# Branch A's scores by pairs of query tiles, the low term as 64-row products

## The chip, the cores and the metric

The kernel runs on one core of a Trainium2 chip. TensorE multiplies, VectorE, ScalarE and GpSimd do the elementwise work, and the DMA queues bring data in and out. The metric is the time of one execution on the device in microseconds; for the kernel before it is 2207.16 us, the median of three runs (2205.43 to 2207.44).

## The reference

One encoder layer is applied to two sequences, a prompt of 1024 tokens and a sample of 512, with 1024 features. All arrays are float32.

```
xn = rmsnorm(x);  z = xn @ W_in -> q_A k_A v_A q_B k_B v_B gate_A gate_B
branch A: 8 query heads of 64, 2 key/value heads; q, k normalised per head and rotated
    s = q @ k.T / 8;  p = softmax(s);  o_A = p @ v          (every query sees every key)
branch B: 8 heads, a window of 8 x 16 neighbours on a grid 64 wide, with a learned bias
mix = (sigmoid(gate_A) * (o_A @ W_pA) + sigmoid(gate_B) * (o_B @ W_pB)) @ W_out
x = x + mix;  x = x + relu(rmsnorm(x) @ W_up)^2 @ W_down;  y = rmsnorm(x)
```

The change touches only `s = q @ k.T` of branch A.

## The kernel before, in words

**Precision.** TensorE multiplies in a reduced form of float32 (fp32r). The kernel keeps accuracy by splitting each operand into a high part, rounded to that form, and a low part, the rest. An ordinary product is then three TensorE products (`mm3`, L157 to L159: high by high, high by low, low by high), summed in PSUM.

**Branch A's operands.** A head has only 64 features, and a product can contract over 128 partitions, so the split is laid out along the partitions. For each key/value group `g` and 128-token tile `tt`, `heads_t` transposes the rotated heads (L446) into a PSUM tile `pt`: four query heads in two 128-partition blocks, and the key head twice, in both halves of the third block. From it ScalarE and VectorE write

- `qT[e]` (e = head's parity): the high part in partitions of half `e` (L451, ScalarE), the low part in the other half (L454, VectorE);
- `kT[:, 0]`: the high part of the keys, in both halves (L452); `kT[:, 1]`: the low part of the keys, in both halves (L460).

**Scores.** One product of `qT[e]` with `kT[:, 0]` over all 128 partitions therefore gives (q high + q low) by k high, and one with `kT[:, 1]` gives (q high + q low) by k low. `s_tile(u, j)` does this for one unit `u` (a head and a block of 512 queries) and one of its four query tiles `j`. It takes a score buffer of two PSUM banks from a pool of two (`big`), and for each block of 512 keys (two of them for the prompt, one for the sample) issues L563 (against the high part, `start=True`) and L564 (against the low part). Then VectorE takes the row maximum (L566), ScalarE the exponential with the row sum (L569), VectorE the reciprocal (L571) and GpSimd scales the probabilities (L572).

**Order of the work.** Units are pipelined: while unit `u` has its probabilities transposed (L606, four 128-column transposes for each 128 keys `kc`), split (L611 ScalarE, L612 VectorE) and multiplied with the values (L582, L583), the score tiles of the next unit are issued at `kc` 0, 1, 3 and 4 of 8 for the prompt and 0, 0, 1 and 2 of 4 for the sample. The products of gate A (L157 to L159, `gpss`) are pulled in between as filling work. This is the order in which the source issues the work; a scheduler then sorts the instructions of each engine anew, by its own estimates, so that the order on an engine can differ.

The sample comes first, then the prompt; each has two key/value groups, so there are four stretches with branch A's scores. Branch B, the projections and the two-layer network follow and are not touched.

Of the kernel before, what the change touches and what calls it, by code (L numbers as in the profile page):

```python
# [10 lines left out]
F32 = mybir.dt.float32  # L11
F32R = mybir.dt.float32r
BF16 = mybir.dt.bfloat16
AF = mybir.ActivationFunctionType
ALU = mybir.AluOpType
AX = mybir.AxisListType

P = 128
D = 1024
NC8 = D // P  # L20
HD = 64
# [39 lines left out]
def encoder(ctx: ExitStack, tc: tile.TileContext, xs, outs, w):  # L61
    nc = tc.nc
    dram = ctx.enter_context(tc.tile_pool(name="dram", bufs=1, space=bass.MemoryType.DRAM))
    cst = ctx.enter_context(tc.tile_pool(name="cst", bufs=1))
    sml = ctx.enter_context(tc.tile_pool(name="sml", bufs=8))
# [17 lines left out]
    def phase(name, bufs=2):  # L83
        return tc.tile_pool(name=name, bufs=bufs, reuse_waits="tile")

    def slot(shape, dt, name, left=False):
        return (s8l if left else s8r).tile(shape, dt, tag="s8", name=name)
# [4 lines left out]
    def mm(name):  # L92
        return pmm.tile([P, 512], F32, tag="mm", name=name)

    def big(name):
        return pbig.tile([P, 1024], F32, tag="big", name=name)
# [40 lines left out]
    def bias_row(r):  # L137
        nc.sync.dma_start(biases[r], shifted[:, :, 7 - r : 23 - r, :])
# [187 lines left out]
    def run(tr, nxt, first):  # L326
        N, x, T, NT, NB = tr.N, tr.x, tr.T, tr.NT, tr.NB
# [8 lines left out]
        fill = Fill()  # L336
# [70 lines left out]
        def load_v(g, alloc):  # L407
            return load_cols(win, 1792 + 256 * g, 256, f"v{N}_{g}", alloc)

        early = {}  # L410
        for g in range(2):
            with phase(f"phR{N}_{g}") as ph:
# [23 lines left out]
                qT = [slot([P, 2, T], F32R, f"qT{N}_{g}_{i}") for i in range(2)]  # L436
                kT = slot([P, 2, T], F32R, f"kT{N}_{g}")
# [3 lines left out]
                def heads_t(tt):  # L441
                    nm = f"{N}_{g}_{tt}"
                    pt = big(f"pq{nm}")[:, :384].rearrange("p (b q) -> p b q", q=P)
                    rrf = rr_of.pop(tt).rearrange("p h d -> p (h d)")
                    for b in range(3):
                        nc.tensor.transpose(pt[:, b, :], rrf[:, b * P : (b + 1) * P], ident)  # L446
                    ts_ = slice(tt * P, (tt + 1) * P)

                    half = (slice(0, HD), slice(HD, P))
                    for e in range(2):  # L450
                        nc.scalar.activation(qT[e][half[e], :, ts_], pt[half[e], 0:2, :], AF.Copy)  # L451
                    nc.scalar.activation(kT[:, 0, ts_], pt[:, 2, :], AF.Copy)  # L452
                    for e in range(2):
                        nc.vector.tensor_tensor(  # L454
                            qT[e][half[1 - e], :, ts_],
                            pt[half[e], 0:2, :],
                            qT[e][half[e], :, ts_].bitcast(F32),
                            op=ALU.subtract,
                        )
                    nc.vector.tensor_tensor(kT[:, 1, ts_], pt[:, 2, :], kT[:, 0, ts_].bitcast(F32), op=ALU.subtract)  # L460
# [15 lines left out]
                for tt in range(NT):  # L476
                    tb, j = divmod(tt, 4)
                    nm = f"{N}_{g}_{tt}"
# [24 lines left out]
                    if tt >= 2:  # L503
                        heads_t(tt - 2)
                    sq = ph.tile([P, 5, HD], F32, tag="sq", name=f"sq{nm}", bufs=1)
                    zq = z[:, :320].rearrange("p (h d) -> p h d", d=HD)
                    ss = sml.tile([P, 8], F32, tag="ss", name=f"ssA{nm}")
# [12 lines left out]
                    u = ph.tile([P, 5, HD], F32, tag="u", name=f"u{nm}", bufs=2)  # L520
# [3 lines left out]
                    for e in range(2):  # L524
# [4 lines left out]
                            op=ALU.mult,  # L529
# [12 lines left out]
                if g == 0:  # L542
                    warm_table(AF.Exp, rr[:, 0, 0:1], f"e{N}")
                values(NT - 1)
                heads_t(NT - 2)
                fill.pull(6)
                heads_t(NT - 1)

            if first and g == 0:
                setup_bias()  # L550
            with phase(f"phA{N}_{g}") as ph:
                units = [(h, qb) for h in range(4) for qb in range(NB)]
                PP = {}

                def s_tile(u, j):
                    h, qb = u
                    nm = f"{N}_{g}_{h}_{qb}_{j}"
                    q0 = (qb * 4 + j) * P
                    lhs = qT[h % 2][:, h // 2, q0 : q0 + P]
                    s = big(f"s{nm}")[:, :T]  # L560
                    for kb in range(NB):
                        ks = slice(kb * 512, kb * 512 + 512)
                        nc.tensor.matmul(s[:, ks], lhs, kT[:, 0, ks], start=True, stop=False)  # L563
                        nc.tensor.matmul(s[:, ks], lhs, kT[:, 1, ks], start=False, stop=True)  # L564
                    nm_ = sml.tile([P, 1], F32, tag="nm", name=f"nm{nm}")
                    nc.vector.tensor_reduce(nm_, s, axis=AX.X, op=ALU.max, negate=True)  # L566
                    p = ph.tile([P, T], F32, tag="P", name=f"p{nm}", bufs=8)
                    l = sml.tile([P, 1], F32, tag="l", name=f"l{nm}")
                    nc.scalar.activation(p, s, AF.Exp, bias=nm_, accum_out=l)  # L569
                    rl = sml.tile([P, 1], F32, tag="rl", name=f"rl{nm}")  # L570
                    nc.vector.reciprocal(rl, l)  # L571
                    nc.gpsimd.tensor_scalar(p, p, rl, 1.0, op0=ALU.mult, op1=ALU.mult)  # L572
                    PP[u, j] = p

                o_of = {}

                def pv(u, kc, hi, lo):
                    h, qb = u
                    if kc == 0:
                        o_of[u] = mm(f"o{N}_{g}_{h}_{qb}")  # L580
                    o = o_of[u]
                    nc.tensor.matmul(o, vhl[:, kc, :], hi, start=(kc == 0), stop=False)  # L582
                    nc.tensor.matmul(o, vhl[:, kc, :], lo, start=False, stop=(kc == NT - 1))  # L583
                    if kc == NT - 1:
                        r0 = (g * 4 + h) * HD
                        finish_o(o, 512, oad[r0 : r0 + HD, qb * 512 : qb * 512 + 512], ph, f"A{N}_{g}_{h}_{qb}")

                for j in range(4):
                    s_tile(units[0], j)
                    fill.pull(2)  # L590
                queue = []
                LAG = 2
                for ui, u in enumerate(units):
                    h, qb = u
                    if first:
                        bias_row(g * 4 + ui)
                        if g == 0 and ui == 1:
                            early["a"] = load_a(1)
                        if g == 0 and ui == 2:
                            early["v"] = load_v(1, slot)  # L600
                    nxt_u = units[ui + 1] if ui + 1 < len(units) else None
                    sdone = 0
                    for kc in range(NT):
                        pt = mm(f"pT{N}_{g}_{h}_{qb}_{kc}")
                        for j in range(4):
                            nc.tensor.transpose(  # L606
                                pt[:, j * P : (j + 1) * P], PP[u, j][:, kc * P : (kc + 1) * P], ident
                            )
                        hi = ph.tile([P, 512], F32R, tag="pth", name=f"pth{N}_{g}_{h}_{qb}_{kc}", bufs=3)
                        lo = ph.tile([P, 512], F32R, tag="ptl", name=f"ptl{N}_{g}_{h}_{qb}_{kc}", bufs=3)  # L610
                        nc.scalar.activation(hi, pt, AF.Copy)  # L611
                        nc.vector.tensor_tensor(lo, pt, hi.bitcast(F32), op=ALU.subtract)  # L612
                        queue.append((u, kc, hi, lo))
                        if nxt_u is not None:
                            while sdone < 4 and kc >= ((0, 1, 3, 4) if NB == 2 else (0, 0, 1, 2))[sdone]:
                                s_tile(nxt_u, sdone)
                                sdone += 1

                        fill.pull(1 if NB == 1 or kc % 4 < 3 else 0)
                        if len(queue) > LAG:  # L620
                            pv(*queue.pop(0))
                fill.drain()
                for item in queue:
                    pv(*item)
# [47 lines left out]
        with phase(f"phB{N}") as ph:  # L672
# [168 lines left out]
            units = [(h, j) for h in range(8) for j in (1, 2, 0, 3)]  # L841
            n = len(units)
            LS, LV = (1, 1) if NB == 2 else (2, 1)
            for i in range(n + LS + LV):
                if i < n - 8:
                    f = (5 if i < LS else 2 + i % 2) if NB == 1 else 5 + (i % 3 > 0)
                else:
                    f = 3 + i % 2 if NB == 1 else 7
# [31 lines left out]
        with phase(f"phG{N}") as ph:  # L880
# [25 lines left out]
            for c in range(NC8):  # L906
# [3 lines left out]
                for tb in range(NB):  # L910
# [4 lines left out]
                    nm = f"{N}_{c}_{tb}"  # L915
# [30 lines left out]
            for half in range(2):  # L946
                wo = wos[half]
                hc = slice(half * 512, half * 512 + 512)
                for tt in range(NT):
                    tb, j = divmod(tt, 4)  # L950
                    nm = f"{N}_{half}_{tt}"
# [35 lines left out]
                    if half == 1:  # L987
# [5 lines left out]
                        else:  # L993
# [6 lines left out]
                            if 3 <= tt <= 5:  # L1000
                                j = tt - 3
# [411 lines left out]
    for i, tr in enumerate(trunks):  # L1413
        run(tr, trunks[i + 1] if i + 1 < len(trunks) else None, i == 0)
# [66 lines left out]
```

## Time and profile before

| | |
|---|---|
| median of three runs | 2207.16 us (2205.43 to 2207.44) |
| the profiled execution | 2204.99 us |
| its span, first to last instruction | 2203.2 us |
| mean granted TensorE clock | 0.993 |
| score products, high keys (L563) | 160 |
| score products, low keys (L564) | 160 |
| transposes of probabilities (L606) | 640 |
| HBM traffic | 263.63 MB read, 87.88 MB written |

The profile shows one execution. The page gives the busy time of each engine, the span in slices and the costliest groups of instructions; further views give a group by line, the busy time of each engine in chosen stretches, the waits of an engine and single instructions in the order of time. PE is TensorE's products, PEld its weight loads, DVE VectorE, ACT ScalarE, POOL GpSimd. In the row of a group come the line in the kernel, the engine and operation, output and inputs by the program's names, the form, the count, the total busy time, the mean duration in ns, and the idle time of the engine ahead of it with what ended it. The record of a product reaches to its modelled end, and successive products overlap, so what a product costs in a stream is the distance between two starts.

### The profile page before, as it was taken

Reading aid. Unit: us, or ns where it says so; the run is one execution under the profiler, and the core shown is the slowest. Engines: PE = TensorE matmul, PEld = TensorE weight load, DVE = VectorE, ACT = ScalarE, POOL = GpSimd, SP = SyncE. Lnnn points to the kernel's source line nnn. Section 1 sums busy time; section 2 is a strip of 40 time slices with the busy share of each in tenths; the row PEclk is TensorE's granted clock in tenths of the full one; section 3 lists DMA queues with packets and bytes.
Section 4 is the critical chain, followed back from the end, with each engine's and each line's share of the span. In section 5 each row is a group of like instructions: output and inputs, shape, how many; then the busy total and the mean of one; then the engine's idle time right before and its main releaser. Section 6 shows DMA issues by size and latency. Waiting matters only on the chain. (4 is left out here: it accounts for less than half of the span.)

```text
span 2203.2 us, 32342 instructions
## 1 busy us (share of the span) xinstructions
PE 2141.6 (97%) x11168; PEld 1873.9 (85%) x11168; DVE 1458.0 (66%) x2823; ACT 1106.2 (50%) x2359; POOL 345.7 (16%) x453
## 2 busy tenths in 40 slices
PE   7999999999999999999999899999999999999998
PEld 7787777888898888888888699998999988888886
DVE  5665566667757755555782777777777777769563
ACT  4654553556636744545540465555655543433352
POOL 2232220333233213222200300003000000000000
PEclk9999999999999999999999999999999999999999
DMA  5535457521122123423463654468544699788561
GB/s 168 156 95 149 142 157 243 202 81 32 44 70 89 39 70 118 118 86 97 144 202 124 234 163 143 155 222 206 173 143 156 219 351 339 235 269 292 166 201 58
DMA packets 318442, 349.72 MB, mean 159 GB/s; under 512 B 31559, under 2 KB 254919, under 8 KB 318279
## 3 DMA queue, kind: packets, MB, share of 16 engines
q1 hardware_dynamic: 277927, 281.58, 40.8%
q10 hardware_dynamic: 35136, 50.61, 6.6%
q0 software_dynamic: 5216, 15.47, 2.5%
q8 instruction: 88, 1.44, 0.3%
q14 instruction: 75, 0.61, 0.1%
HBM read 263.63 MB, written 87.88 MB: 160 GB/s over the span
## 5 line engine op out<-in xcount | busy, mean ns | idle before, releaser
L159 PE MATMUL dn<-wd,al 128*128 128x512 f32 x624 | 242.8, 389 | 0.0
L158 PE MATMUL dn<-wd,ah 128*128 128x512 f32 x624 | 242.8, 389 | 0.0
L157 PE MATMUL dn<-wd,ah 128*128 128x512 f32 x624 | 242.7, 389 | 0.0
L1034 ACT ACTIVATE ah<-ar 128x512 fp32r<-128x512 f32 x168 | 104.4, 628 | 212.8 <-PE dn L158 196.0
L1035 DVE TENSOR_TENSOR al<-ar,ah 128x512 fp32r<-128x512 f32 x168 | 115.9, 698 | 77.1 <-ACT ah L1034 66.4
L157 PEld LDWEIGHTS dn<-wd,ah 128*128 128x128 f32 x624 | 117.1, 188 | 24.4
L159 PEld LDWEIGHTS dn<-wd,al 128*128 128x128 f32 x624 | 117.1, 188 | 24.3
L158 PEld LDWEIGHTS dn<-wd,ah 128*128 128x128 f32 x624 | 117.1, 188 | 24.2
L612 DVE TENSOR_TENSOR ptls<-pTs,pths 128x512 fp32r<-128x512 f32 x160 | 107.5, 686 | 38.1 <-ACT pths L611 37.6
L611 ACT ACTIVATE pths<-pTs 128x512 fp32r<-128x512 f32 x160 | 94.2, 598 | 74.9 <-PE pTs L606 72.9
L572 POOL TENSOR_SCALAR ps<-ps,rls 128x1024 f32<-128x1024 f32 (+1 forms) x96 | 96.1, 1003 | 215.0 <-DVE rls L571 208.6
L566 DVE TENSOR_REDUCE nms<-ss 128x1 f32<-128x1024 f32 (+1 forms) x96 | 99.5, 1040 | 26.3 <-PE ss L564 26.2
L144 POOL TENSOR_TENSOR rs_f<-ms_f,mhalf 128x1 f32<-128x1 f32 x12 | 7.4, 615 | 652.4 <-DVE ms_f L142 652.4
L157 PE MATMUL gpss<-xs_0h,w_gs 128*128 128x512 f32 x256 | 105.9, 414 | 3.0 <-ACT sgs L355 1.3
L569 ACT ACTIVATE ps<-ss,nms 128x1024 f32<-128x1024 f32 (+1 forms) x96 | 93.3, 973 | 23.7 <-DVE nms L566 21.3
L606 PEld LDWEIGHTS pTs<-ident,ps 128*128 128x128 f32 x640 | 78.1, 140 | 29.7 <-POOL ps L572 5.6
L159 PE MATMUL gpss<-xs_0h,w_gs 128*128 128x512 f32 x256 | 101.1, 395 | 0.1
L606 PE MATMUL pTs<-ident,ps 128*128 128x128 f32 x640 | 99.0, 274 | 2.0 <-DVE ptls L612 1.0
L158 PE MATMUL gpss<-xs_0l,w_gs 128*128 128x512 f32 x256 | 100.9, 394 | 0.0
L157 PE MATMUL ua<-B,A 128*128 128x384 f32 x256 | 86.4, 338 | 5.6 <-ACT A L1034 5.6
L783 POOL TENSOR_SCALAR pbs<-pbs,rlbs 128x384 f32<-128x384 f32 (+1 forms) x96 | 56.4, 592 | 225.3 <-DVE rlbs L782 219.1
L1034 ACT ACTIVATE A<-S 128x512 fp32r<-128x512 f32 x128 | 76.1, 623 | 28.5 <-DVE S L1079 25.8
(279 smaller groups left out, 6428.1 us busy)
## 6 DMA issues: line engine op xcount, KB each, us to landing
ar<-ud SPq DMA_DIRECT2D x120, 512.0 KB
br<-in_w_mlp_down_dram SPq DMA_DIRECT2D x72, 512.0 KB
rawu<-in_w_mlp_up_dram SPq DMA_DIRECT2D x64, 512.0 KB
ud<-c ACTq DMA_DIRECT2D x128, 192.0 KB
raw_gs<-in_w_in_dram SPq DMA_DIRECT2D x32, 512.0 KB
zgs<-sgs ACTq DMA_DIRECT2D x48, 256.0 KB
ud<-cs SPq DMA_DIRECT2D x64, 192.0 KB
raw_os<-in_w_out_dram SPq DMA_DIRECT2D x16, 512.0 KB
```

The lines of the kernel that those rows point to most:

```text
L157: nc.tensor.matmul(out, ah, bh, start=start, stop=False, **kw)
L158: nc.tensor.matmul(out, ah, bl, start=False, stop=False, **kw)
L159: nc.tensor.matmul(out, al, bh, start=False, stop=stop, **kw)
L566: nc.vector.tensor_reduce(nm_, s, axis=AX.X, op=ALU.max, negate=True)
L569: nc.scalar.activation(p, s, AF.Exp, bias=nm_, accum_out=l)
L572: nc.gpsimd.tensor_scalar(p, p, rl, 1.0, op0=ALU.mult, op1=ALU.mult)
L606: nc.tensor.transpose(pt[:, j * P : (j + 1) * P], PP[u, j][:, kc * P : (kc + 1) * P], ident)
L611: nc.scalar.activation(hi, pt, AF.Copy)
L612: nc.vector.tensor_tensor(lo, pt, hi.bitcast(F32), op=ALU.subtract)
L783: nc.gpsimd.tensor_scalar(p, p, rl, 1.0, op0=ALU.mult, op1=ALU.mult)
L1034: nc.scalar.activation(hi, src, AF.Copy)
L1035: nc.vector.tensor_tensor(lo, src, hi.bitcast(F32), op=ALU.subtract)
```

## The change

Each query tile now has its high and low parts in halves that depend on the parity of the tile as well as of the head: on odd tiles `d = e ^ 1`, so the high part lies in the other half. `s_tile` becomes `s_pair(u, jj)`, which handles query tiles `2*jj` and `2*jj + 1` at once, with both score buffers. It first issues the products against the high keys for both tiles, over all 128 partitions as before. Then, for each block of keys, it issues the products against the low keys for the two tiles in turn, each only over the 64 partitions that hold the tile's high query part: one tile's product uses partitions 0 to 63, the other's 64 to 127, and they write different PSUM banks. The product of the low query part with the low key part is no longer computed. The maximum, exponential, reciprocal and scaling follow for the one tile and then the other, as before. Pairs are issued at `kc` 0 and 3 of 8 for the prompt and 0 and 1 of 4 for the sample, and the filling work at the start of a stretch is pulled four steps after each pair instead of two after each tile.

```
                     for e in range(2):
-                        nc.scalar.activation(qT[e][half[e], :, ts_], pt[half[e], 0:2, :], AF.Copy)
+                        d = e ^ (tt & 1)
+                        nc.scalar.activation(qT[e][half[d], :, ts_], pt[half[e], 0:2, :], AF.Copy)
                     nc.scalar.activation(kT[:, 0, ts_], pt[:, 2, :], AF.Copy)
                     for e in range(2):
+                        d = e ^ (tt & 1)
                         nc.vector.tensor_tensor(
-                            qT[e][half[1 - e], :, ts_],
+                            qT[e][half[1 - d], :, ts_],
                             pt[half[e], 0:2, :],
-                            qT[e][half[e], :, ts_].bitcast(F32),
+                            qT[e][half[d], :, ts_].bitcast(F32),
                             op=ALU.subtract,
                         )
...
-                def s_tile(u, j):
+                def s_pair(u, jj):
                     h, qb = u
...
-                    for kb in range(NB):
-                        ks = slice(kb * 512, kb * 512 + 512)
-                        nc.tensor.matmul(s[:, ks], lhs, kT[:, 0, ks], start=True, stop=False)
-                        nc.tensor.matmul(s[:, ks], lhs, kT[:, 1, ks], start=False, stop=True)
...
+                    ss = []
+                    for j in (2 * jj, 2 * jj + 1):
+                        q0 = (qb * 4 + j) * P
+                        s = big(f"s{N}_{g}_{h}_{qb}_{j}")[:, :T]
+                        ss.append((j, q0, s))
+                        for kb in range(NB):
+                            ks = slice(kb * 512, kb * 512 + 512)
+                            lhs = qT[h % 2][:, h // 2, q0 : q0 + P]
+                            nc.tensor.matmul(s[:, ks], lhs, kT[:, 0, ks], start=True, stop=False)
+                    for kb in range(NB):
+                        ks = slice(kb * 512, kb * 512 + 512)
+                        for j, q0, s in ss:
+                            d = (h + j) % 2
+                            hs = slice(HD * d, HD * d + HD)
+                            nc.tensor.matmul(
+                                s[:, ks], qT[h % 2][hs, h // 2, q0 : q0 + P], kT[hs, 1, ks], start=False, stop=True
+                            )
...
-                for j in range(4):
-                    s_tile(units[0], j)
-                    fill.pull(2)
+                for jj in range(2):
+                    s_pair(units[0], jj)
+                    fill.pull(4)
...
-                            while sdone < 4 and kc >= ((0, 1, 3, 4) if NB == 2 else (0, 0, 1, 2))[sdone]:
-                                s_tile(nxt_u, sdone)
+                            while sdone < 2 and kc >= ((0, 3) if NB == 2 else (0, 1))[sdone]:
+                                s_pair(nxt_u, sdone)
                                 sdone += 1
```

More of the change, by code (lines that the diff above doesn't have):

```diff
@@ L553, in run @@
                 PP = {}
-                def s_tile(u, j):
+                def s_pair(u, jj):
                     h, qb = u
[L557 to L560, printed above, removed]
+                    ss = []
[7 more added lines that the diff above has]
+                            nc.tensor.matmul(s[:, ks], lhs, kT[:, 0, ks], start=True, stop=False)
@@ L561, in s_tile @@
                     for kb in range(NB):
                         ks = slice(kb * 512, kb * 512 + 512)
[L563 to L573, printed above, removed]
+                        for j, q0, s in ss:
[4 more added lines that the diff above has]
+                            )
@@ new lines, in s_pair @@
+                    for j, q0, s in ss:
+                        nm = f"{N}_{g}_{h}_{qb}_{j}"
+                        nm_ = sml.tile([P, 1], F32, tag="nm", name=f"nm{nm}")
+                        nc.vector.tensor_reduce(nm_, s, axis=AX.X, op=ALU.max, negate=True)
+                        p = ph.tile([P, T], F32, tag="P", name=f"p{nm}", bufs=8)
+                        l = sml.tile([P, 1], F32, tag="l", name=f"l{nm}")
+                        nc.scalar.activation(p, s, AF.Exp, bias=nm_, accum_out=l)
+                        rl = sml.tile([P, 1], F32, tag="rl", name=f"rl{nm}")
+                        nc.vector.reciprocal(rl, l)
+                        nc.gpsimd.tensor_scalar(p, p, rl, 1.0, op0=ALU.mult, op1=ALU.mult)
+                        PP[u, j] = p
```

## The prediction

> **What bounds the kernel now.** I read the page's busy shares first, then busy time by stretch, then TensorE's waits inside these stretches, then single products in the order of time.
>
> ```profile
> span 2203.2 us, 32342 instructions
> PE 2141.6 (97%) x11168; PEld 1873.9 (85%) x11168; DVE 1458.0 (66%) x2823; ACT 1106.2 (50%) x2359; POOL 345.7 (16%) x453
> ```
>
> TensorE is busy for 97% of the span. That is an average, so the stretches that hold branch A's scores come next. The score products come in four stretches, two key/value groups of the 512-token sequence and two of the 1024-token one; the row of their line gives the first and the last start, and the table the stretches.
>
> ```profile
> L563 PE MATMUL ss<-kTs,qTs x160: 387/397/501, 62.1 to 783.8; 128*128 128x512 f32 x160
> ...
> core 0: us, PE busy (x) PEld busy (x) DVE busy (x) ACT busy (x) POOL busy (x), PEclk, DMA share, GB/s
> 62.00:95.00 33.00, 32.40 (x158) 24.97 (x159) 25.39 (x56) 24.30 (x52) 9.71 (x14) 1.00 0.42 120
> 139.00:172.00 33.00, 32.34 (x162) 25.36 (x163) 24.55 (x53) 23.77 (x52) 10.83 (x16) 1.00 0.37 108
> 481.00:600.00 119.00, 117.81 (x628) 96.21 (x629) 88.28 (x139) 78.75 (x139) 36.88 (x32) 1.00 0.12 37
> 675.00:800.00 125.00, 124.91 (x670) 102.05 (x670) 90.86 (x143) 82.82 (x145) 36.75 (x32) 1.00 0.17 49
> sum 310.00, PE 307.46 PEld 248.58 DVE 229.08 ACT 209.63 POOL 94.17; mean PE 76.87 PEld 62.15 DVE 57.27 ACT 52.41 POOL 23.54
> ```
>
> TensorE is busy for 307.5 of 310 us at a granted clock of 1.00; VectorE and ScalarE have about a quarter to a third left. So in these stretches a microsecond added to or taken from TensorE moves the end by a microsecond, until another engine becomes late. The waits in the longest of them:
>
> ```profile
> engine line waited for: us in total, times, longest us
> PE ss L563 <- DVE kTs L460: 1.2, 1, 1.2
> PE pTs L606 <- DVE ptls L612: 1.0, 2, 0.7
> ```
>
> Two microseconds, none of it for a score buffer. What a product costs is not its record but the distance from its start to the next start:
>
> ```profile
> 744.72 0.39 PE L563 MATMUL ss<-kTs,qTs 128*128 128x512 f32 x1
> 744.73 0.19 PEld L564 LDWEIGHTS ss<-kTs,qTs 128*128 128x128 f32 x1
> 744.95 0.40 PE L564 MATMUL ss<-kTs,qTs 128*128 128x512 f32 x1
> 744.96 0.19 PEld L157 LDWEIGHTS gpss<-xs_0h,w_gs 128*128 128x128 f32 x1
> 745.19 0.39 PE L157 MATMUL gpss<-xs_0h,w_gs 128*128 128x512 f32 x1
> 745.42 0.40 PE L158 MATMUL gpss<-xs_0l,w_gs 128*128 128x512 f32 x1
> ...
> 746.11 0.58 PEld L606 LDWEIGHTS pTs<-ident,ps 128*128 128x128 f32 x4
> 746.34 0.60 PE L606 MATMUL pTs<-ident,ps 128*128 128x128 f32 x4
> 746.66 0.19 PEld L563 LDWEIGHTS ss<-kTs,qTs 128*128 128x128 f32 x1
> 746.69 0.48 PE L563 MATMUL ss<-kTs,qTs 128*128 128x512 f32 x1
> 746.77 0.19 PEld L564 LDWEIGHTS ss<-kTs,qTs 128*128 128x128 f32 x1
> 747.01 0.40 PE L564 MATMUL ss<-kTs,qTs 128*128 128x512 f32 x1
> ```
>
> Two things are to be seen. Products of 512 columns start every 0.23 us (744.72, 744.95, 745.19), though each record lasts 0.39: the last 0.16 us of one lies beside the next. And the weights of the next product are loaded while the present one runs (the load of 744.96 starts with the product of 744.95), so the 0.19 us of a load cost nothing.
>
> **The change part by part.** Durations that follow are means of these groups.
>
> ```profile
> L563 PE MATMUL ss<-kTs,qTs 128*128 128x512 f32 x160 | 68.4, 427 | 3.3 <-DVE kTs L460 3.3
> L564 PE MATMUL ss<-kTs,qTs 128*128 128x512 f32 x160 | 64.2, 401 | 0.0
> L606 PE MATMUL pTs<-ident,ps 128*128 128x128 f32 x640 | 99.0, 274 | 2.0 <-DVE ptls L612 1.0 <-POOL ps L572 0.3 <-DVE rls L571 0.2
> L566 DVE TENSOR_REDUCE nms<-ss 128x1 f32<-128x1024 f32 x64 | 77.7, 1217 | 16.5 <-PE ss L564 16.5
> L569 ACT ACTIVATE ps<-ss,nms 128x1024 f32<-128x1024 f32 x64 | 71.4, 1115 | 17.7 <-DVE nms L566 15.4 <-DVE rls L571 2.0
> L569 ACT ACTIVATION_READ_ACCUMULATOR ps<-ss,nms 128x1 f32 x96 | 19.0, 198 | 0.0
> L454 DVE TENSOR_TENSOR qTs<-pqs,qTs 64x256 fp32r<-64x256 f32 x48 | 20.3, 422 | 2.1 <-ACT kTs L452 1.4
> L451 ACT ACTIVATE qTs<-pqs 64x256 fp32r<-64x256 f32 x48 | 18.1, 377 | 5.0 <-PE pqs L446 3.4 <-DVE w_gs L152 1.3
> L740 DVE TENSOR_TENSOR kBs<-pkbs,kBs 64x512 fp32r<-64x512 f32 x48 | 33.1, 689 | 38.4 <-ACT kBs L738 37.9
> L738 ACT ACTIVATE kBs<-pkbs 64x512 fp32r<-64x512 f32 x48 | 28.5, 594 | 40.0 <-PE pkbs L159 30.9 <-DVE kBs L740 8.5
> ```
>
> *What stays.* The 160 first products (L563) and the 160 second products (L564) keep their number, their 512 columns and a weight load each; so do the reduces, exponentials and normalisations. The only work that can vanish is time shared by two of the 160 products that shrink from 128 to 64 rows. Run one at a time they would cost what they cost now, 160 x 0.23 = 36.8 us.
>
> *How many can share.* The scheduler sorts each engine's work, so I count in the order of TensorE's instructions of the built kernel. With T for a product on rows 0 to 63, B for rows 64 to 127, the 160 stand in 76 unbroken runs: 29 of one product, 10 of two on the same half, 13 TB, 11 of the form TBT and 13 TBTB. If neighbours on different halves run together, a TB or TBT run saves one place and a TBTB run two: 13 + 11 + 26 = 50 places, not the 80 that the source suggests. In the other cases the second buffer's first product, or another stage's, was sorted in between.
>
> *What a shared place saves.* At most the whole 0.23 us: 50 x 0.23 = 11.4 us (0.227 unrounded). At least nothing, if halves don't run side by side. Between these, the second product needs its own weights. The nearest row is the run of four transposes, each with a load of its own: (0.60 - 0.27) / 3 = 0.11 us from one to the next. I take it that the second product starts one such load later, so a place saves 0.23 - 0.11 = 0.12 us and 50 save 5.9 us. The Trainium skill (TensorE: Matmul & The Clock Gate, Part 3) has products on different row groups start about 4 ns apart; by that the 50 places would save about 11.2 us and the forecast would come out some 5 us lower. No run before the change has two products on different rows, so the trace neither agrees nor differs.
>
> *What a change of shape costs.* In the old kernel every product uses all 128 rows (the "128*128" in each row). Each of the 76 runs is entered from a 128-row product and left to one: 152 changes. No row shows such a change. Lower bound: the change between transposes and products, which costs nothing: after the four transposes of 746.34 the next two products start at 746.69 and 747.01, and 0.67 us for four transposes and one product is 4 x 0.11 + 0.23. A gain is excluded, since the plain 0.23 us is never beaten by products of 512 columns. Upper bound: the array runs empty (0.39 - 0.23 = 0.16 us) and the new weights are only loaded then (0.19 us), 0.35 us. I take 0.16 us: the tail is what two successive products of different shape would share in the array, which no row shows being shared, while the load goes into a place that the running product doesn't use, as the load of 744.96 does. That is 152 x 0.16 = 24.6 us (0.162 unrounded), with 0 and 53 us as ends.
>
> *Buffers.* A score tile fills one of two buffers, and now two tiles are filled nearly together. A buffer is free after reduce, exponential and accumulator read: 1.22 + 1.12 + 0.20 = 2.53 us, and the second of a pair waits for the first one's reduce, 3.75 us. Laying both kernels' TensorE orders out at 0.23 us a product and 0.11 us a transpose, the places where buffer or probabilities come too late add up to about 1.3 us before and 2.0 us after. Behind such a wait on TensorE's queue stand transposes, value products and gate products alike, so it costs in full: +0.7 us.
>
> *Query halves.* On odd tiles ScalarE's 24 copies (L451, 377 ns) write the other half of the partitions and VectorE's 24 subtractions (L454) read inputs on different halves. L738 and L740 do both already, at 594 and 689 ns for 64x512 against 377 and 422 for 64x256, which is no dearer per element. Nothing is added. DMAs, their queues and GpSimd's instructions keep their number.
>
> *Sum.* -5.9 + 24.6 + 0.7 = +19.4 us on the profiled execution's 2204.99 us. The median of the runs, 2207.16 us, lies 2.2 us above it; on that I forecast 2226.
>
> **The rivals.**
>
> *Sharing without a price (faster).* The 64-row products flow in behind the 128-row ones with no gap, as products do behind transposes. Then 5.9 to 11.4 us vanish: 2196 to 2201, say 2199. For it: TensorE is full in these stretches, so all of it would show. Against it: the rows show free succession only where the shape stays 128x128. It decides once a change of shape costs less than 5.9 / 152 = 0.04 us (0.07 if places save in full). The Trainium skill (TensorEngine Tiling (Array Packing), Key Properties) speaks against it: changing the tiling mode, unlike changing the tile, drains the engine, and it gives no time for that. No run here shows it yet.
>
> *Empty array and exposed load (much slower).* Nothing of the new shape is loaded before the old has left: 152 x 0.35 = 53 us, less 5.9, so about 2254. For it: a 64-row load and a 128-row load would have to sit in one spare set of weights. Against it: loads run well ahead wherever the trace can be looked at.
>
> *The halves do not run side by side and changes are free (same).* The order changes and nothing else: 2207 to 2208. The middle ground belongs here too, where price and saving cancel (0.04 to 0.07 us a change).
>
> *The buffers become the bound.* With both filled together, TensorE would stand before a pair, with VectorE's second reduce (1.22 us) as the cause. Across 48 pairs even half a microsecond each would be 24 us. Against it: the layout above leaves 2.5 us or more to nearly every reuse, and VectorE is busy 229 of 310 us. I count it within the forecast's spread.
>
> **How the numbers follow.** Below 0.2%, about 4.4 us, a difference can't be told from none here (the three runs span 2 us). Sharing without a price gets 0.31; no change and cancelling 0.13; the forecast, with 0.09 to 0.22 us a change, 2214 to 2236, 0.43; the dear change above it 0.13. So faster 0.31, same 0.13, slower 0.56. The range takes in the faster rival's low end and leaves the dearest changes out: 2196 to 2243, some 0.15 outside. The forecast's own range is 2214 to 2236.
>
> **What will show it.** In the order of time, pairs on different halves should start 0.11 us apart rather than 0.23 (a saved place), and the first 64-row product of a run, and the first 128-row one behind it, should start about 0.39 us after their forerunners rather than 0.23 (the price of a change). The four stretches should together take 19 us more, all else unchanged. If pairs start together and their neighbours stay at 0.23 us, the faster rival is right. If gaps exceed 0.5 us, loads are exposed. If TensorE's waits name L566's or L569's successor in front of score products for more than 3 us, the buffers were misjudged.

## The result, and the profile after

The changed kernel takes 2223.34 us (median of 6 runs, 2220.94 to 2228.24) against 2207.30 us of the kernel before beside it: a ratio of 1.0077, 95% interval 1.0067 to 1.0088. It is 0.8% slower. The forecast was 2226 us, slower.

The page's head for the changed kernel shows the same number of TensorE products and a span that is 16.0 us longer.

```profile
span 2219.2 us, 32334 instructions
PE 2161.5 (97%) x11168; PEld 1861.2 (84%) x11168; DVE 1459.5 (66%) x2823; ACT 1108.2 (50%) x2359; POOL 346.1 (16%) x453
```

Where the 16 us lie is shown by the four stretches, each from its first score product to its last product with the values. First the kernel before, then the changed one; after the bounds come the length and each engine's busy time with its instructions.

```profile
core 0: us, PE busy (x) PEld busy (x) DVE busy (x) ACT busy (x) POOL busy (x), PEclk, DMA share, GB/s
62.10:103.20 41.10, 40.58 (x201) 31.31 (x201) 31.13 (x66) 28.94 (x61) 11.07 (x16) 1.00 0.49 140
139.00:179.80 40.80, 40.05 (x201) 31.59 (x202) 29.49 (x60) 27.20 (x58) 12.11 (x17) 1.00 0.45 125
481.10:610.50 129.40, 128.31 (x686) 104.80 (x687) 93.61 (x146) 83.34 (x147) 36.88 (x32) 1.00 0.12 36
674.70:803.00 128.30, 128.17 (x685) 104.85 (x686) 91.95 (x144) 84.18 (x148) 37.39 (x33) 1.00 0.17 51
```

```profile
62.20:107.00 44.80, 44.78 (x206) 31.34 (x207) 31.21 (x66) 29.43 (x61) 11.08 (x16) 1.00 0.43 132
142.00:185.10 43.10, 43.02 (x201) 30.51 (x202) 29.42 (x60) 27.48 (x58) 13.23 (x17) 1.00 0.44 120
487.10:621.50 134.40, 134.14 (x686) 98.54 (x687) 94.28 (x146) 83.32 (x147) 36.07 (x32) 1.00 0.12 35
685.70:819.80 134.10, 134.00 (x685) 98.57 (x686) 93.10 (x144) 84.28 (x148) 37.58 (x33) 1.00 0.17 48
```

The stretches sum to 339.6 us before and 356.4 us after: +16.8 us, all of the difference and 0.8 more. The long stretches hold the same number of products (686 and 685; the first short one holds five more), the clock stays at 1.00, and VectorE and ScalarE keep their busy time. TensorE is busy throughout, but its weight loads are busy for less: in the third stretch 98.5 us instead of 104.8. Part of that is that loads overlap. The rows of the second score product's loads, before and after, show both that and a new idle time ahead of them:

```profile
L564 PEld LDWEIGHTS ss<-kTs,qTs 128*128 128x128 f32 x160 | 30.5, 190 | 3.5
L576 PEld LDWEIGHTS ss<-kTs,qTs 64*128 64x128 f32 x160 | 17.8, 184 | 22.3 <-issue 22.1
```

The 160 loads of 184 ns would fill 29 us one by one and fill 17.8. The idle time ahead of them grew from 3.5 to 22.3 us. The waits of the weight loads list it with the others of its kind (columns: who waited for whom, us in total, times, longest):

```profile
engine line waited for: us in total, times, longest us
PEld ss L576 <- issue: 22.1, 74, 0.4
PEld gpss L157 <- issue: 7.4, 24, 0.4
PEld os L598 <- issue: 4.6, 17, 0.4
```

L576 is the 64-row product. 74 times, and there are 76 runs, its load came after 0.30 us of idle time on average, in which it waited for nothing that the profile names. The groups of the two score products:

```profile
L570 PE MATMUL ss<-kTs,qTs 128*128 128x512 f32 x160 | 53.1, 412 | 3.3 <-DVE kTs L463 3.3
L576 PE MATMUL ss<-kTs,qTs 64*128 64x512 f32 x160 | 45.8, 466 | 0.0
```

And in the order of time, a run of one 64-row product and then a run of four:

```profile
487.88 0.39 PE L159 MATMUL gpss<-xs_0h,w_gs 128*128 128x512 f32 x1
487.88 0.19 PEld L570 LDWEIGHTS ss<-kTs,qTs 128*128 128x128 f32 x1
488.10 0.40 PE L570 MATMUL ss<-kTs,qTs 128*128 128x512 f32 x1
488.43 0.18 PEld L576 LDWEIGHTS ss<-kTs,qTs 64*128 64x128 f32 x1 [0.36 <-issue]
488.43 0.49 PE L576 MATMUL ss<-kTs,qTs 64*128 64x512 f32 x1
488.85 0.19 PEld L157 LDWEIGHTS gpss<-xs_0h,w_gs 128*128 128x128 f32 x1 [0.24 <-issue]
488.85 0.50 PE L157 MATMUL gpss<-xs_0h,w_gs 128*128 128x512 f32 x1
488.96 0.19 PEld L158 LDWEIGHTS gpss<-xs_0l,w_gs 128*128 128x128 f32 x1
489.19 0.40 PE L158 MATMUL gpss<-xs_0l,w_gs 128*128 128x512 f32 x1
...
489.42 0.40 PE L159 MATMUL gpss<-xs_0h,w_gs 128*128 128x512 f32 x1
...
515.58 0.30 PEld L576 LDWEIGHTS ss<-kTs,qTs 64*128 64x128 f32 x4 [0.37 <-issue]
515.59 0.74 PE L576 MATMUL ss<-kTs,qTs 64*128 64x512 f32 x4
...
516.25 0.50 PE L157 MATMUL gpss<-xs_0h,w_gs 128*128 128x512 f32 x1
...
516.59 0.40 PE L158 MATMUL gpss<-xs_0l,w_gs 128*128 128x512 f32 x1
```

Between products of one shape the distances are 0.23 us (489.19 to 489.42). From the last 128-row product to the 64-row one they are 0.33 (488.10 to 488.43), and the load of the 64-row weights starts not with the product ahead of it, as the load of 487.88 does, but 0.33 us later, with its own product. From there to the next 128-row product 0.42 us pass, whose load is late too (488.85), and to the one after it 0.34. Together 1.09 us for three steps that would take 0.68: the run of one costs 0.41 us more than a 128-row product in its place. The run of four lies between the starts 515.59 and 516.25, 0.66 us for four products: they went two by two. All 50 neighbours on different halves did so: in the trace's starts the second comes 3 or 4 ns after the first in 44 of them and 1 to 6 ns in the rest. The second pair of such a run then starts 0.33 us after the first.

So three theories were ready. **Theory A:** the price belongs to the change between 128-row and 64-row products: the array empties, about 0.10 us, and then a weight load stands in the open, 0.107 us (the load of 488.96 starts that long after the product of 488.85, whose own load came late), 0.2 us a change. Side by side, products share a whole place of 0.227 us. **Rival B:** filling two buffers together is what costs. **Rival C:** the price belongs to each 64-row product.

### The profile page after: what moved, and what is told of

The parts are those of the page before. It is cut to its first block, busy times and chain, and to the rows that moved or that the text cites. A ratio compares the mean times of both kernels' runs of the same rounds, so it can differ in the third digit from the quotient of the medians.

```text
span 2219.2 us, 32334 instructions
## 1 busy us (share of the span) xinstructions
PE 2161.5 (97%) x11168; PEld 1861.2 (84%) x11168; DVE 1459.5 (66%) x2823; ACT 1108.2 (50%) x2359; POOL 346.1 (16%) x453
## 5 line engine op out<-in xcount | busy, mean ns | idle before, releaser
L157 PE MATMUL gpss<-xs_0h,w_gs 128*128 128x512 f32 x256 | 110.0, 430 | 3.4 <-ACT sgs L355 1.3
L159 PE MATMUL gpss<-xs_0h,w_gs 128*128 128x512 f32 x256 | 102.3, 400 | 0.1
L1050 ACT ACTIVATE A<-S 128x512 fp32r<-128x512 f32 x128 | 76.1, 623 | 28.0 <-DVE S L1095 25.5
```

The source lines that it names most:

```text
L157: nc.tensor.matmul(out, ah, bh, start=start, stop=False, **kw)
L159: nc.tensor.matmul(out, al, bh, start=False, stop=stop, **kw)
L1050: nc.scalar.activation(hi, src, AF.Copy)
```

## The experiments

**The same order with 128 rows.** One product differs:

```
-  nc.tensor.matmul(s[:, ks], qT[h % 2][hs, h // 2, q0 : q0 + P], kT[hs, 1, ks], start=False, stop=True)
+  nc.tensor.matmul(s[:, ks], qT[h % 2][:, h // 2, q0 : q0 + P], kT[:, 1, ks], start=False, stop=True)
```

> The changed kernel with its low-key products over all 128 rows again, so the pairs, their order and both score buffers stay and no product changes shape. Theory A (the time is lost where the array changes between 128-row and 64-row products): all of the loss goes, and what the order itself does remains; the gaps at changes add up to 19.9 us in the trace while the span grew by 16.0, so I expect 2203 to 2208 us. Rival B (the loss comes from the pairing: two buffers filled together, reduces and exponentials late): it stays near 2223 us.

Measured: 2209.85 us, ratio 1.0006 (0.9997 to 1.0015), 2 us above the range I gave. The loss is gone, so it came from the 64-row products and not from the pairing; rival B falls. The pairing itself costs 2 us by the medians and at most 3.3 by the interval, which does not tell it from nothing.

**Both products of a pair on the same half.**

```
-  d = e ^ (tt & 1)          # twice
+  d = e
...
-  d = (h + j) % 2
+  d = h % 2
```

> The changed kernel without the swap on odd query tiles, so both products of a pair lie on the same half of the array and can't run side by side; 76 runs of 64-row products as before. Theory A: the 76 runs keep their 0.41 us each and the 50 shared places of 0.227 us are lost, 11.4 us more than the changed kernel: 2233 to 2236 us. Were the sharing worth only 0.12 us a place, as I had predicted, it would be 2229; were nothing shared, 2223.

Measured: 2233.23 us, ratio 1.0111 (1.0094 to 1.0127). Without the swap the kernel is 9.9 us slower than the changed one by the medians, 50 places of 0.198 us, and 7.5 us slower by the two ratios, 0.15 us a place. The intervals lie apart, so the sharing is real. Its size is not settled by these times: the 2229 us of a place worth 0.12 us is a ratio of 1.0097, inside the interval. The traces settle it, below.

**Every 64-row product alone,** in the kernel before (the low query part times the low key part is left out, as in the changed kernel):

```
-  nc.tensor.matmul(s[:, ks], lhs, kT[:, 1, ks], start=False, stop=True)
+  hs = slice(HD * (h % 2), HD * (h % 2) + HD)
+  nc.tensor.matmul(s[:, ks], qT[h % 2][hs, h // 2, q0 : q0 + P], kT[hs, 1, ks], start=False, stop=True)
```

> The kernel before with its low-key product cut to 64 rows and nothing else: 160 64-row products, every one between 128-row products, so 160 runs of one and 320 changes of shape. Theory A (0.207 us a change: 0.10 until the array has emptied and 0.107 of a weight load that is no longer hidden): 160 x 0.41 = 66 us, 2265 to 2275 us. Rival C (the price belongs to each 64-row product and not to the change; then the changed kernel's 16 us and its 11.4 us of sharing make 0.17 us a product): 160 x 0.17 = 27 us, 2234 us.

Measured: 2266.22 us, ratio 1.0266 (1.025 to 1.0281). The number of 64-row products is the same, 160, but they stand in 160 runs instead of 76, and the loss is 58 us. The kernel with both products on one half shares no place either, and loses 25.5 us by the medians with its 76 runs: the loss goes with the runs and not with the products. Rival C's figure is missed by 32 us, and it falls.

**The 64-row products of a pair kept together.**

```
-  for kb in range(NB):
-      ...
-          nc.tensor.matmul(...)
+  with tc.high_priority():
+    for kb in range(NB):
+        ...
+          tc.keep_in_program_order(nc.tensor.matmul(...))
```

> The changed kernel with the 64-row products of a pair pinned behind the pair's 128-row ones and put ahead of other work, so that they stand together: 48 runs (32 of four products on alternating halves, 16 of two) and 80 shared places. Theory A: 48 x 0.41 - 80 x 0.227 = +1.7 us against the kernel before, less the 3 us that the order seems to give, plus what waiting for both buffers costs: 2204 to 2211 us. Rival C: 27 - 18 = +9 us, 2216. Rival B (pairing itself is dear): 2223 or more, since the pairs are tied closer.

Measured: 2213.48 us, ratio 1.0028 (1.0019 to 1.0037), 2.5 us above theory A's range and 2.5 below rival C's figure. With 80 shared places the kernel is 10 us faster than the changed one, but not as fast as before. That left a question: is a run dearer here, or does the tied order cost? The next kernel has exactly this order.

**The kept-together order with 128 rows.** The edit is that of the first experiment, made in the kernel just shown.

> The grouped kernel, product for product in the same order on TensorE, with the low-key products over all 128 rows. It tells whether the grouped kernel's 6 us come from the tied order or from the 64-row products. By the comparison of equal orders so far a run costs 0.365 us and a shared place saves 0.222 us; theory A then gives 48 x 0.365 - 80 x 0.222 = -0.2 us for the products of the grouped kernel, so this one lies where that one did, 2212 to 2215 us: the order is what costs. Rival: changes are dearer when runs stand at other places; then this lies near 2208 to 2210.

Measured: 2210.98 us, ratio 1.0014 (1.0005 to 1.0023), between the two figures. The tied order alone costs about 3 us against the kernel before. The remaining 2.5 us are not clear of noise, since the intervals of the two kernels overlap; in the two traces, compared product by product below, the difference does not lie at the runs.

**Longer runs.**

```
+  lhs = qT[h % 2][:, h // 2, q0 : q0 + P]
+  nc.tensor.matmul(s[:, 0:512], lhs, kT[:, 0, 0:512], start=True, stop=False)
...
-  for kb in range(NB):
+  for i, kb in [(0, 1), (1, 1), (1, 0)] if NB == 2 else [(1, 0)]:
...
-  kT[hs, 1, ks], start=False, stop=True
+  kT[hs, i, ks], start=i == 0, stop=i == 1
```

> The grouped kernel with longer runs: for the prompt the high-key products of the second block of keys are 64-row products too (high query part only; the low query part times the high keys is left out for these keys). 48 runs as before, 32 of them of six products on alternating halves, so 112 shared places instead of 80. Theory A (price per change, none per product): 32 places more at 0.222 us, 7.1 us less than the grouped kernel: 2204 to 2208 us. Rival C (0.17 us per 64-row product): 64 products more, 10.9 - 7.1 = 3.8 us more than it, 2216 to 2219 us.

Measured: 2207.21 us, ratio 0.9997 (0.9988 to 1.0006): 6.3 us less than the grouped kernel, where A said 7.1 less and C 3.8 more. A longer run has no price beyond its two ends. One of its runs, after the score product ahead of it:

```profile
512.71 0.40 PE L568 MATMUL ss<-kTs,qTs 128*128 128x512 f32 x1
513.03 0.96 PE L576 MATMUL ss<-kTs,qTs 64*128 64x512 f32 x6
513.93 0.66 PE L623 MATMUL pTs<-ident,ps 128*128 128x128 f32 x4
```

Six products take the 0.90 us from 513.03 to 513.93, 0.24 us more than the four of 515.59 above.

**A change of shape by columns.**

```
-  nc.tensor.matmul(o, vhl[:, kc, :], hi, start=(kc == 0), stop=False)
-  nc.tensor.matmul(o, vhl[:, kc, :], lo, start=False, stop=(kc == NT - 1))
+  nc.tensor.matmul(o, vhl[:, kc, :], hi, start=(kc == 0), stop=(kc == NT - 1), ...)
+  nc.tensor.matmul(o[0:HD, :], vhl[:, kc, 0:HD], lo, start=False, stop=(kc == NT - 1), ...)
```

> The kernel before with another change of shape: of the two products with the values, the one with the low part of the probabilities uses only the 64 columns of the values' high part (the product of the two low parts is left out). 160 such products, each between others of 128 columns, so 320 changes of shape by columns instead of rows. Theory A widened to every change of shape: the same as the 160 runs of the tile64 kernel or a little less, since a load of 64 columns is shorter: +45 to +60 us, 2252 to 2268. Theory A for rows alone: 2207 us.

Measured: 2206.43 us, ratio 0.9996 (0.9987 to 1.0005). Nothing was lost. In the order of time:

```profile
751.65 0.40 PE L564 MATMUL ss<-kTs,qTs 128*128 128x512 f32 x1
...
751.88 0.39 PE L582 MATMUL os<-pths,vhls 128*128 128x512 f32 x1
751.89 0.13 PEld L583 LDWEIGHTS os<-ptls,vhls 128*64 128x64 f32 x1
...
752.11 0.40 PE L583 MATMUL os<-ptls,vhls 128*64 128x512 f32 x1
752.12 0.19 PEld L563 LDWEIGHTS ss<-kTs,qTs 128*128 128x128 f32 x1
752.35 0.39 PE L563 MATMUL ss<-kTs,qTs 128*128 128x512 f32 x1
```

The 64-column product keeps the 0.23 us to both neighbours, and its load runs beside the product ahead of it. The wide form of theory A, any change of shape, falls: the price was paid where the number of rows changed, and not where the number of active columns did.

**Equal orders compared.** Five kernels have partners with exactly the same order of all 11,168 products on TensorE. From the start-to-start distances of both traces, summed, in us:

```
kernel against partner     runs  shared places  at the runs  rest of stretches  outside
samehalf  - pair128          76        0           +27.7          -3.1           +3.5
changed   - pair128          76       50           +16.6          -1.7           -0.6
grouped   - grouped128       48       80            -0.1          +1.4           +1.0
tile64    - before          160        0           +60.9          -2.6           +3.1
col64     - before          160        0            -0.2          -0.1           +0.9
```

(samehalf is the kernel with both products on one half, pair128 the same order with 128 rows, tile64 the one with every 64-row product alone; "at the runs" reaches from the last product ahead of a run to the first behind the one that follows it.) The first row gives 27.7 / 76 = 0.365 us a run, the fourth 60.9 / 160 = 0.381. The first two give (27.7 - 16.6) / 50 = 0.222 us a shared place. With these, the third should be 48 x 0.365 - 80 x 0.222 = -0.2, and is -0.1: the grouped kernel's 64-row products just break even, and its 2.3 us against its partner lie elsewhere. Nothing outside the stretches was changed, so the last column, up to 3.5 us, shows how far two executions can differ without a cause in the edit. A run of four on alternating halves saves 0.07 us on average there, a run of two costs 0.14.

## Why the prediction was right, and where it was right by luck

The direction, the place and the mechanism hold: TensorE bounds the four stretches, the whole loss lies in them, and it is the change between 128-row and 64-row products that costs. The total, +19.4 predicted and +16.0 us in the profiled span, came out of three terms of which two were missed in opposite directions, so that it came out so close is partly luck.

- *Shared places.* The count, 50, stands. The size, 0.12 us, was too small: it measured 0.222 us, so the term was -11.1 us and not -5.9. The step that failed is that the second product would wait for a weight load. The loads of both halves run at the same time (515.58: four loads in 0.30 us, the first two together), and the two products mostly start 3 to 4 ns apart. That agrees with the Trainium skill (TensorE: Matmul & The Clock Gate, Part 3), which has products on different row groups start about 4 ns apart; the forecast went by the row of the transposes instead.
- *Changes of shape.* 152 x 0.162 = 24.6 us was predicted; equal orders give 76 x 0.365 = 27.7 us, 0.18 us a change. The size was nearly right, its make-up wrong. I had the array's whole tail of 0.16 us, with the load hidden; the records show about 0.10 us until the next shape starts and then a load of 0.107 us in the open. What I took from the load of 744.96, that a load goes into a spare place, held here only where the number of rows did not change from one product to the next. Standing free, tail and load add up to 0.41 us a run in the records. Against a partner with the same order the mean is 0.365 us: 0.385 us for the 35 runs with 512-column products all around, where the partner has 0.045 us beyond 0.227 us a product itself, and 0.31 us for the 14 runs that two transposes follow.
- *Buffers.* +0.7 us was predicted. The 128-row partner's span is 1.7 us longer than that of the kernel before, 2.1 us by the medians, which its interval does not tell from none. TensorE's waits in the changed kernel's third stretch name nothing but the keys:

```profile
engine line waited for: us in total, times, longest us
PE ss L570 <- DVE kTs L463: 1.2, 1, 1.2
```

- *Query halves.* Nothing was added: VectorE and ScalarE are busy 1459.5 and 1108.2 us, 1.5 and 2.0 us more than before.

The sum with measured sizes: +1.7 (order) + 27.7 - 11.1, less 1.7 us that the rest of the stretches gained and 0.6 outside, is the +16.0 us of the span. It has to be, since all the terms are parts of the same traces; what it shows is how the 16 us divide. Had only the sharing been sized right, the forecast would have been 2221; had only the load been put in the open at its 0.107 us, with the tail kept at 0.16, it would have been some 16 us higher, 2243.

Of the rivals, *sharing without a price* was half true: the sharing came in full, and the price decided. Its point of decision, 0.07 us a change with whole places, lies below the 0.18 measured. The *exposed load* rival was right that the load comes late and had the size too large: 0.18 us a change and not 0.35. If a load in the open costs the 0.107 us to the next one, and not the 0.19 us of its record, that is part of it. The sign set for it, gaps above 0.5 us, appeared at no end of a run (0.33 and 0.42 us at the run above, 0.49 us at most), though the loads were late; and the gaps of 0.39 us that the forecast expected on both sides were 0.33 us ahead of a run and 0.42 and 0.34 us behind it. *Not side by side* is refuted by the kernel on one half, *buffers as the bound* by the 128-row partner.

The Trainium skill (TensorEngine Tiling (Array Packing), Key Properties) says that changing the tiling mode drains the engine. For rows the trace fits that: 0.33 us instead of 0.23 to the first 64-row product, and no load runs ahead. For columns it is open: the same page lists 128x64 as a mode of its own, and 320 changes between 128 and 64 active columns cost -0.2 us at the products, but the trace does not show whether the chip changed its mode there.

What stays open: whether the 0.10 us is the array emptying or the load's own path, since no kernel here separates tail and load; and whether the 2.5 us by which the grouped kernel lies above its partner are more than noise.

No version beats the kernel before. At 0.365 us a run and 0.222 us a place a run must share two places to gain at all, and the low-key products of a pair in two score buffers share two at most. The longer runs match the kernel before (0.9997) only by leaving part of the products out.

## What to carry to other kernels

In these runs two 64-row products on different halves of the array, in different banks, ran together and saved nearly a whole product's place (0.222 of 0.227 us here); but each entry into and exit from such a run cost nearly as much as a product (0.18 us against 0.227). So count runs in the order in which the engine gets them, not pairs in the source. At these sizes a run pays only where it shares two places or more, and the cutting apart by the scheduler decides much: with the same 160 products the cost at the runs was +16.6 us in 76 runs and -0.1 in 48. Columns are another matter: here a product on half the columns between full ones cost nothing extra, and saved nothing.

## What the runs showed that I had not expected

In these traces no 64-row load was issued ahead across a change of shape: 22.1 us of idle time stand ahead of such loads, 74 times, without any releaser in the profile, and the record of the first load of each of the 76 runs starts with that of its product. And half-row and half-column products differ altogether in this: +60.9 us at 160 runs of the one, -0.2 at 160 of the other. What looked like one property, the shape of a product, is not one.
